# First values of a two-layer decoder trunk projected from the raw first tile, with the norm weights applied by feature

## The chip, the cores and the metric

The kernel runs on one core of a Trainium2 chip. The metric is the device time of one execution in microseconds. Three timed runs of the kernel before gave 706.67, 707.9 and 708.45; one more execution was profiled.

## What is computed

Two decoder layers run over 512 positions of 1024 features. What matters here is the start of layer 0 and the way its three branches share one normalised input:

```python
def rms_norm(x, g):
    y = xf * lax.rsqrt(jnp.mean(xf * xf, axis=-1, keepdims=True) + EPS)
    return y * g
...
h = rms_norm(x, norm_g)                       # norm_g: 1024 weights, one per feature
a_u, a_v, a_g, b_q, b_k, b_v, b_g, m_q, m_g = split_cols(h @ w_in, EVEN_SPLITS)
...
y_m = memory_attention(m_q, mem_n, m_wkv, m_qnorm, m_knorm) * silu(m_g)
return x + concatenate([y_a, y_b, y_m]) @ w_out
```

The factor of a position (its rsqrt) is the same for all features, so a product of one position's row with the weights can take it before the product or after it. The factor of a feature (its norm weight) must come in before the sum over features.

## The kernel before

The 512 positions are four tiles of 128 rows, x_t[0] to x_t[3]. A projection needs the input with features on the partitions, so `h_tile` makes each tile of h in these steps: ScalarE squares it with a running sum (L412), GpSimd makes the factor of each row (`rstd`, L370 and L372), VectorE multiplies the tile by that factor and by the norm weights (L417; the weights stand in `gain0`, one row of 4 KB that a DMA copies to all 128 partitions, L328), TensorE transposes eight blocks of 128x128 (L399), and `split` writes each half of four blocks as two numbers: ScalarE the rounded high part (L376), VectorE the remainder, the low part (L377). Each weight unit of 128x1024 numbers (512 KB, L384) is split in the same way; with an engine given, VectorE makes the low part (L377), without one GpSimd makes it in two instructions of 512 columns (L386 on ScalarE and L389 on GpSimd). A product of two such operands is three matmuls (`mm3`, L402 to L404).

The first projection is `b_v`, the values of the differential attention: 4 tiles by 8 feature blocks by 3, so 96 matmuls of 512 columns, from four weight units that are loaded ahead (`loaded`). The projection for `a_values` follows, 96 more from four further units.

All DMAs are issued by SyncE in one order. At the start this is: two halves of x_t[0], the norm weights, then in turn a weight unit and a tile of x, then three small tables (vec, tab, col). Raw weight units stand in three pages, so a fourth DMA of a unit waits until the low part of an earlier one is made. Pages of SBUF and banks of PSUM are handed out by small allocators (`Arena`), oldest first; a scheduler sets the order of each engine's instructions when the kernel is built, so that a change at one place can shift the order at others.

In the middle of the kernel the fill work of layer 0 ends with the keys and values of the memory tokens for both layers (`mem_kv`); its keys are normalised (`head_norm`, `to_keys`, L517) and transposed. Then `m_attn` (scores L601 and L602, exponentials L607, scaling L609 and L610) is merged with the first part of the output projection (`out_part`), whose products are L402 to L404 again. Around there SyncE also loads the weights of the second norm (`gain1`, L328).

Of the kernel before, what the change touches and what calls it, by code (L numbers as in the profile page):

```python
# [24 lines left out]
F32R = mybir.dt.float32r  # L25
# [6 lines left out]
P = 128  # L32
# [82 lines left out]
def layout(inputs):  # L115

    g = {k: np.asarray(v) for k, v in inputs.items()}
    wall = np.empty((NUNITS, P, DM), np.float32)
    for name, (src, kind, c) in UNITS.items():
        w = g[src]  # L120
        i, cnt = UIDX[name]
        if kind == "t":
            wall[i] = w[:, c:c + P].reshape(KT, P, P).transpose(1, 0, 2).reshape(P, DM)
        elif kind == "n":
            ww = np.concatenate([w[:, a:a + n] for a, n in c], axis=1)
            n = ww.shape[1]
# [12 lines left out]
    col[:, 5:9] = g["l1_c_norm"].reshape(4, P).T  # L139
    col[:, 9:13] = g["l1_c_conv_b"].reshape(4, P).T  # L140
    col[:, 13:137] = g["l1_c_conv_w"].reshape(31, 4, P).transpose(2, 1, 0).reshape(P, 124)
    for j, nm in enumerate("kv"):
        pe = g[f"l1_d_cmp_pos_{nm}"].reshape(16, 2, 64)
        col[:, 137 + 16 * j:153 + 16 * j] = pe.transpose(1, 2, 0).reshape(P, 16)
    w1 = np.stack([g[f"l1_d_cmp_w1_{nm}"].reshape(16, P, P).transpose(1, 0, 2).reshape(P, 2048) for nm in "kv"])
    w2 = np.concatenate([g[f"l1_d_cmp_w2_{nm}"] for nm in "kv"], axis=1)
    wsT = np.ascontiguousarray(g["l0_a_ws"].transpose(2, 0, 1).reshape(P, 512))
    norms = np.stack([g["mem_norm"], g["l0_norm"], g["l1_norm"]])
    return dict(x=g["x"].reshape(S, DM), mem=g["mem"].reshape(256, DM), wall=wall, wqb=wqb,
                vec=vec, bs=g["l0_a_bs"].reshape(1, 512), col=col, w1=w1, w2=np.ascontiguousarray(w2), wsT=wsT, norms=norms,  # L150
                tab=tables())


# [132 lines left out]
def emit(ctx, tc, nc, D, out):  # L286
# [28 lines left out]
    def tok(i):  # L315
        return slice(i * P, (i + 1) * P)
# [15 lines left out]
    x_t[0] = x_sc([P, DM])  # L332
    for a in range(2):
        dma(x_t[0][:, a * 512:(a + 1) * 512], D["x"][tok(0), a * 512:(a + 1) * 512])
    gain0 = load_gain(1, start_sc)
    coff = [0]

    def C(shape):
# [7 lines left out]
            v = v.rearrange("p (a b c) -> p a b c", a=shape[1], b=shape[2])  # L346
        return v

    ident = C([P, P])
    make_identity(nc, ident)  # L350
    mhalf = C([P, 32])
# [16 lines left out]
    def rstd(sc, ss, scale, n, eps=EPS, parts=P):  # L368
        v = sc([P, n])[:parts]
        G.tensor_scalar(v, ss, scale, eps, MUL, ADD)  # L370
        r = sc([P, n])[:parts]
        G.tensor_tensor(r, v, mhalf[:parts, :n], ALU.pow)  # L372
        return r
# [29 lines left out]
        mm(o, lh, rl, start=False, stop=False)  # L403
        mm(o, ll, rh, start=False, stop=last)  # L404

    def h_tile(xt, gain, hs, tk, parts=1):
        with SC() as sc:
            xs = sc([P, DM])
            ss = sc([P, 2])
            cols = [slice(a * DM // parts, (a + 1) * DM // parts) for a in range(parts)]  # L410
            for a, c in enumerate(cols):
                act(xs[:, c], xt[:, c], AF.Square, accum_out=ss[:, a:a + 1])  # L412
            if parts == 2:
                G.tensor_tensor(ss[:, 0:1], ss[:, 0:1], ss[:, 1:2], ADD)
            r = rstd(sc, ss[:, 0:1], 1.0 / DM, 1)
            for c in cols:
                V.scalar_tensor_tensor(xs[:, c], xt[:, c], r, gain[:, c], MUL, MUL)  # L417
            for b in range(2):
                with SC() as pc:
                    p = pc.ps("t", [P, 4, P])  # L420
                    for k in range(4):
                        tr(p[:, k, :], xs[:, (4 * b + k) * P:(4 * b + k + 1) * P])
                    split(p, hs[0][b][:, :, tk], hs[1][b][:, :, tk])
# [18 lines left out]
            w += [(h[:, j * n:(j + 1) * n], l[:, j * n:(j + 1) * n]) for j in range(nk)]  # L442
        return w

    def proj_N(hs, units, order, n, loaded=()):


        order = list(order)
        per = S // n
        groups = [order[a:a + per] for a in range(0, len(order), per)]  # L450
        psc = [SC() for _ in groups]
        ps = [c.ps("d", [P, per, n]) for c in psc]
        k0 = 0
        for m, part in enumerate(units):
            with (loaded[m][0] if m < len(loaded) else SC()) as wsc:
                w = loaded[m][1] if m < len(loaded) else unit_parts(wsc, part, n)
                for a, g in enumerate(groups):
                    for b, i in enumerate(g):
                        for j, (wh, wl) in enumerate(w):
                            k = k0 + j  # L460
                            mm3(ps[a][:, b, :], hs[0][k // 4][:, k % 4, tok(i)], hs[1][k // 4][:, k % 4, tok(i)],
                                wh, wl, k + b == 0, k == KT - 1 and b == len(g) - 1)
                    if k0 + len(w) == KT:
                        for b, i in enumerate(g):
                            yield i, ps[a][:, b, :]
                        psc[a].close()
                k0 += len(w)
# [281 lines left out]
    for i in range(NT):  # L749
        if i:  # L750
            x_t[i] = x_sc([P, DM])
            dma(x_t[i], D["x"][tok(i), :])
        wsc = SC()
        loaded.append((wsc, unit_parts(wsc, first[i], 512, V)))
    dma(vec, bc(D["vec"], [P, VLEN]))
    dma(tab, D["tab"])
    dma(col, D["col"])
    hsc = SC()
    h0 = [[hsc([P, 4, S], F32R) for _ in range(2)] for _ in range(2)]
    for i in range(NT):  # L760
        h_tile(x_t[i], gain0, h0, tok(i), 1 if i else 2)
    x_sc.close()


# [144 lines left out]
    bV = [bsc([P, 2, 512]) for _ in range(2)]  # L909

    def b_v():
        for i, p in proj_N(h0, first, range(NT), 512, loaded):
            act(bV[i // 2][:, i % 2, :], p, AF.Copy)
            yield UT

    yB = [ysc([P, 2, S]) for _ in range(2)]

# [103 lines left out]
                (out_part(0, [(yA[0], 0, 2), (yA[1], 2, 2)], rev), FILLM0)))  # L1021
    msc.close()
    g1sc = SC()
    gain1 = load_gain(2, g1sc)
    banks(*P_DENSE)
    drain(out_part(0, [(yB[0], 4, 2), (yB[1], 6, 2), (yM[0], 8, 2)], rev))
    ysc.close()
# [345 lines left out]
FILLG, FILLC, GLU1 = 0.8, 0.12, 1  # L1373


ARRAYS = ["x", "mem", "wall", "wqb", "vec", "bs", "col", "w1", "w2", "wsT", "norms", "tab"]


def build(shapes):
# [13 lines left out]
```

## Time and profile before

| what | value |
|---|---|
| timed runs | 706.67, 707.9, 708.45 us (median 707.9) |
| profiled execution, its own time | 706.9 us |
| its span in the profile | 705.2 us |
| TensorE busy | 665.2 us, 94% |
| VectorE busy | 492.9 us, 70% |
| ScalarE busy | 376.7 us, 53% |
| GpSimd busy | 392.9 us, 56% |

The span is what the profile shows; 1.7 us of the profiled execution's time lie outside it. TensorE is called PE in rows (PEld is its weight load), VectorE DVE, ScalarE ACT, GpSimd POOL, SyncE SP. A row of a timeline gives start and length in us, then engine, line, operation and operands, and in brackets the idle time ahead of it and what ended that.

### The profile page before, as it was taken

Reading aid. Unit: us, or ns where it says so; the run is one execution under the profiler, and the core shown is the slowest. Engines: PE = TensorE matmul, PEld = TensorE weight load, DVE = VectorE, ACT = ScalarE, POOL = GpSimd, SP = SyncE. Lnnn points to the kernel's source line nnn. Section 1 sums busy time; section 2 is a strip of 40 time slices with the busy share of each in tenths; the row PEclk is TensorE's granted clock in tenths of the full one; section 3 lists DMA queues with packets and bytes.
Section 4 is the critical chain, followed back from the end, with each engine's and each line's share of the span. In section 5 each row is a group of like instructions: output and inputs, shape, how many; then the busy total and the mean of one; then the engine's idle time right before and its main releaser. Section 6 shows DMA issues by size and latency. Waiting matters only on the chain.

```text
span 705.2 us, 11053 instructions
## 1 busy us (share of the span) xinstructions
PE 665.2 (94%) x3819; PEld 563.5 (80%) x3819; DVE 492.9 (70%) x1204; ACT 376.7 (53%) x846; POOL 392.9 (56%) x414
## 2 busy tenths in 40 slices
PE   4999989999999997899999999999999999999997
PEld 3789989888888875688888888777777888788875
DVE  4705678667666865675274978999967776998773
ACT  5345345556455675563253568642446666676541
POOL 3467887575436767442473879966664523421650
PEclk9999999999999999799999999999999999999999
DMA  8532135463313253212132411104121101120121
GB/s 303 187 116 94 60 87 151 140 171 128 108 57 121 90 190 134 95 63 88 51 104 85 151 66 60 61 1 149 32 89 59 61 31 60 51 70 1 61 76 74
DMA packets 22376, 66.56 MB, mean 94 GB/s; under 512 B 3504, under 2 KB 3760, under 8 KB 22320
## 3 DMA queue, kind: packets, MB, share of 16 engines
q1 hardware_dynamic: 22320, 65.86, 28.8%
q8 instruction: 30, 0.49, 0.3%
q14 instruction: 26, 0.21, 0.1%
HBM read 57.46 MB, written 2.10 MB: 84 GB/s over the span
## 4 chain that ended last, share of the span: by engine, by line
PE 71%; DVE 11%; POOL 7%; ACT 4%; DMA 4%; issue 3%; SPq 0%; POOLq 0%; ACTq 0%; DVEq 0%
PE banks L403 18%; PE banks L402 18%; PE banks L404 18%; PE banks L399 5%; PE banks L927 4%; DMA arena_f<-in_wall_dram 3%; POOL arena_r L389 3%; POOL arena_f L372 3%; PE banks L1212 2%; DVE arena_r L377 2%; PE banks L965 2%; ACT arena_r L386 1%; DVE arena_f L929 1%; PE banks L1088 1%; PE banks L1182 1%
## 5 line engine op out<-in xcount | busy, mean ns | idle before, releaser
L389 POOL TENSOR_TENSOR arena_r<-arena_f,arena_r 128x512 fp32r<-128x512 f32 (+1 forms) x174 | 228.5, 1337 | 187.4 <-ACT arena_r L386 183.8
L402 PE MATMUL banks<-arena_r 128*128 128x512 f32 (+2 forms) x784 | 290.0, 374 | 5.1 <-ACT arena_r L386 2.3
L403 PE MATMUL banks<-arena_r 128*128 128x512 f32 (+2 forms) x784 | 289.9, 370 | 3.2 <-POOL arena_r L389 2.1
L404 PE MATMUL banks<-arena_r 128*128 128x512 f32 (+2 forms) x784 | 288.3, 370 | 0.0
L402 PEld LDWEIGHTS banks<-arena_r 128*128 128x128 f32 x784 | 148.4, 190 | 30.3 <-ACT arena_r L386 3.7
L403 PEld LDWEIGHTS banks<-arena_r 128*128 128x128 f32 x784 | 148.7, 190 | 26.9 <-POOL arena_r L389 3.9
L404 PEld LDWEIGHTS banks<-arena_r 128*128 128x128 f32 x784 | 148.4, 189 | 22.6 <-DVE arena_r L377 0.3
L386 ACT ACTIVATE arena_r<-arena_f 128x1024 fp32r<-128x1024 f32 (+2 forms) x87 | 91.2, 1049 | 76.2 <-PE banks L403 21.6
L399 PE MATMUL banks<-const,arena_f 128*128 128x128 f32 x507 | 80.5, 277 | 13.9 <-DVE arena_f L417 9.7
L929 DVE CUSTOM_DVE_ANT_0 arena_f<-banks,const 128x512 f32<-128x512 f32 (+3 forms) x128 | 60.4, 484 | 33.4 <-PE banks L927 26.7
L377 DVE TENSOR_TENSOR arena_r<-banks,arena_r 128x512 fp32r<-128x512 f32 (+1 forms) x112 | 66.8, 608 | 22.9 <-ACT arena_r L376 22.5
L399 PEld LDWEIGHTS banks<-const,arena_f 128*128 128x128 f32 x507 | 60.9, 143 | 25.3 <-DVE arena_f L417 10.2
L376 ACT ACTIVATE arena_r<-banks 128x512 fp32r<-128x512 f32 (+1 forms) x112 | 57.2, 532 | 41.8 <-PE banks L399 28.8
L372 POOL TENSOR_TENSOR arena_f<-arena_f,const 128x4 f32<-128x4 f32 (+3 forms) x60 | 68.0, 1136 | 3.6
L1261 DVE SCALAR_TENSOR_TENSOR banks<-arena_f,const,banks 128x482 f32<-128x482 f32 (+14 forms) x90 | 66.1, 734 | 1.3
L927 PE MATMUL banks<-arena_r 128*128 128x512 f32 (+7 forms) x192 | 50.6, 337 | 4.4 <-DVE arena_f L929 2.1
L958 ACT ACTIVATE arena_f<-arena_f 128x512 f32<-128x512 f32 (+3 forms) x64 | 35.8, 561 | 26.4 <-DVE arena_f L929 25.9
L1189 ACT ACTIVATE arena_f<-arena_f 128x256 f32<-128x256 f32 (+3 forms) x64 | 35.7, 559 | 26.1 <-DVE arena_f L929 25.3
L657 DVE TENSOR_TENSOR arena_f<-arena_f,banks 128x512 f32<-128x512 f32 x40 | 27.0, 684 | 24.0 <-PE banks L404 23.7
L574 POOL TENSOR_SCALAR arena_f<-arena_f 128x512 f32<-128x512 f32 (+3 forms) x32 | 19.9, 627 | 39.6 <-DVE arena_f L1191 33.7
L927 PEld LDWEIGHTS banks<-arena_r 128*128 128x128 f32 (+1 forms) x192 | 32.7, 189 | 10.6 <-DVE arena_f L929 4.7
L1259 POOL TENSOR_TENSOR arena_f<-arena_f 128x482 f32<-128x482 f32 (+29 forms) x30 | 37.8, 1258 | 2.2 <-ACT arena_f L1258 0.6
(177 smaller groups left out, 810.6 us busy)
## 6 DMA issues: line engine op xcount, KB each, us to landing
arena_f<-in_wall_dram SPq DMA_DIRECT2D x88, 512.0 KB, 3.3
arena_r<-arena_r SPq DMA_DIRECT2D x96, 64.0 KB, 2.0
arena_f<-in_x_dram SPq DMA_DIRECT2D x7, 512.0 KB, 6.2
arena_f<-in_w_dram SPq DMA_DIRECT2D x4, 512.0 KB, 3.7
out_dram<-arena_f SPq DMA_DIRECT2D x8, 256.0 KB, 2.0
arena_f<-in_norms_dram SPq DMA_DIRECT2D x3, 512.0 KB, 4.4
arena_f<-in_mem_dram SPq DMA_DIRECT2D x2, 512.0 KB, 3.3
arena_f<-in_wqb_dram SPq DMA_DIRECT2D x2, 420.0 KB, 3.3
```

The costliest lines, as they stand in the source:

```text
L372: G.tensor_tensor(r, v, mhalf[:parts, :n], ALU.pow)
L376: act(h, src, AF.Copy)
L377: (eng or V).tensor_tensor(l, src, f32(h), SUB)
L386: act(h, raw, AF.Copy)
L389: G.tensor_tensor(l[:, c], raw[:, c], f32(h[:, c]), SUB)
L399: nc.tensor.transpose(o, i, ident[:k, :k])
L402: mm(o, lh, rh, start=first, stop=False)
L403: mm(o, lh, rl, start=False, stop=False)
L404: mm(o, ll, rh, start=False, stop=last)
L927: mm(t[:, a % per, :], q, k[:, :w], start=b == 0, stop=b == len(qk) - 1)
L929: V.tensor_tensor_reduce(e[a], t[:, a % per, :], cmask[:, S - w:], -1.0, -NEG, ADD, ALU.min, nm[:, a:a + 1])
L1261: V.scalar_tensor_tensor(acc[:, z:], hc[:, :S - z], cw[:, f, k:k + 1], acc[:, z:], MUL, ADD)
```

## The change

The first tile is transposed raw. `t_tile` transposes four blocks, multiplies them in PSUM by the norm weights, which now stand as a column per feature block in `gcol` (128 partitions by 8, a DMA of 4 KB), and splits them. The first tile goes through it twice: once raw into `own`, which only `b_v` uses, and once multiplied by its row factor into h0 as the others. For the products from `own` the row factor comes in when ScalarE copies the values of tile 0 out of PSUM (`scale=r_first`). For all four tiles the row factor is applied by GpSimd (`G.tensor_scalar`, 128x1024) instead of VectorE, and the norm weights by VectorE after the transposes. The DMA that copied the row of norm weights to all partitions is gone at the start. Of the four weight units of `b_v`, the second and the fourth have their low part made by GpSimd now.

```diff
-    gain0 = load_gain(1, start_sc)
...
+    gcol = C([P, KT])
+    dma(gcol, D["gcol"])
...
+    def t_tile(xs, hs, tk):
+        for b in range(2):
+            with SC() as pc:
+                p = pc.ps("t", [P, 4, P])
+                for k in range(4):
+                    tr(p[:, k, :], xs[:, (4 * b + k) * P:(4 * b + k + 1) * P])
+                V.tensor_tensor(p, p, bc(gcol[:, 4 * b:4 * b + 4].unsqueeze(2), [P, 4, P]), MUL)
+                split(p, hs[0][b][:, :, tk], hs[1][b][:, :, tk])
...
-        loaded.append((wsc, unit_parts(wsc, first[i], 512, V)))
+        loaded.append((wsc, unit_parts(wsc, first[i], 512, None if i % 2 else V)))
...
+    ownsc = SC()
+    own_t = ownsc([P, 4, S], F32R)
+    own = [[own_t[:, 2 * a + b, :].rearrange("p (k t) -> p k t", k=4) for b in range(2)] for a in range(2)]
+    t_tile(x_t[0], own, tok(0))
     for i in range(NT):
-        h_tile(x_t[i], gain0, h0, tok(i), 1 if i else 2)
+        with SC() as sc:
+            xs = sc([P, DM])
+            r = rms(sc if i else ownsc, xs, x_t[i], 1 if i else 2)
+            if i == 0:
+                r_first = r
+            G.tensor_scalar(xs, x_t[i], r, 0.0, MUL, ADD)
+            t_tile(xs, h0, tok(i))
...
-        for i, p in proj_N(h0, first, range(NT), 512, loaded):
-            act(bV[i // 2][:, i % 2, :], p, AF.Copy)
+        for i, p in proj_N(h0, first, range(NT), 512, loaded, own):
+            act(bV[i // 2][:, i % 2, :], p, AF.Copy, scale=1.0 if i else r_first)
```

The order of the instructions changes with it at two places; lines of the changed kernel are a little larger (L399 becomes L401, L402 to L404 become L404 to L406, L377 L379, L389 L391, L372 L374, L384 L386, L328 L329, L324 L325, L601 and L602 become L616 and L617, L517 L532). On TensorE at the start of the program stood, before, eight transposes behind VectorE's scaled tile and then the first products:

```order
L399 MATMUL banks<-const,arena_f 128x128 [waits DVE_49]
L399 MATMUL banks<-const,arena_f 128x128 x3
L402 MATMUL banks<-arena_r 128x512 [waits Activation_49]
L403 MATMUL banks<-arena_r 128x512 [waits DVE_49]
L404 MATMUL banks<-arena_r 128x512 [waits DVE_49]
```

Now the raw tile's transposes wait for the DMA of x alone, and the transposes of the scaled tile come in behind the first product:

```order
L401 MATMUL banks<-const,arena_f 128x128 [waits DMAHW0_49,Pool_49]
L401 MATMUL banks<-const,arena_f 128x128 x3
L401 MATMUL banks<-const,arena_f 128x128 [waits DMAHW1_49]
L401 MATMUL banks<-const,arena_f 128x128 x3
L404 MATMUL banks<-arena_r 128x512 [waits Activation_49]
L401 MATMUL banks<-const,arena_f 128x128 [waits DVE_49,Pool_49]
L401 MATMUL banks<-const,arena_f 128x128 x3
L405 MATMUL banks<-arena_r 128x512 [waits DVE_49]
```

What moved: the first transposes left VectorE's queue, and eight more transposes stand among the products of tile 0. GpSimd, at the same place, had only the row factors (L370, L372) before its first low parts; now its queue holds the row scaling (L786) and the low part of a weight unit (L391) between them:

```order
L374 TENSOR_TENSOR arena_f<-arena_f,const 128x1 [waits Pool_49]
L786 TENSOR_SCALAR arena_f<-arena_f 128x1024 [waits DMAHW1_49,DMAHW0_49,Pool_49]
L372 TENSOR_SCALAR arena_f<-arena_f 128x1 [waits Activation_49]
L374 TENSOR_TENSOR arena_f<-arena_f,const 128x1 [waits Pool_49]
L786 TENSOR_SCALAR arena_f<-arena_f 128x1024 [waits DMAHW4_49,Pool_49]
L391 TENSOR_TENSOR arena_r<-arena_f,arena_r 128x512 [waits DMAHW5_49,Activation_49]
L391 TENSOR_TENSOR arena_r<-arena_f,arena_r 128x512
```

The second place is the entry into the memory attention. On SyncE the load of the second norm's weights stood before a weight unit; before:

```order
L328 DMA arena_f_61<-in_norms_dram 128x1024 [waits PE_49]
L384 DMA arena_f_61<-in_wall_dram 128x1024 [waits DMAHW1_49,DMAHW5_49,Activation_49,Pool_49]
L324 DMA arena_f_61<-in_x_dram 128x1024 [waits DMAHW6_49,PE_49]
```

In the changed kernel that unit is issued ahead of it:

```order
L386 DMA arena_f_61<-in_wall_dram 128x1024 [waits DMAHW1_49,DMAHW4_49,Activation_49,Pool_49]
L329 DMA arena_f_61<-in_norms_dram 128x1024 [waits DMAHW5_49,PE_49]
L325 DMA arena_f_61<-in_x_dram 128x1024 [waits PE_49]
```

On TensorE, behind the first scores (L601 and L602), the second set of scores was followed by the products of the output projection; before:

```order
L601 MATMUL banks<-arena_r 128x256 [waits Activation_49]
L602 MATMUL banks<-arena_r 128x256
L402 MATMUL banks<-arena_r 128x512 [waits DVE_49]
L403 MATMUL banks<-arena_r 128x512 [waits Pool_49]
```

Now four transposes, two sets of scores and four more transposes (those of the memory keys, behind VectorE's L532) stand ahead of these products:

```order
L401 MATMUL banks<-const,arena_f 128x128 [waits DVE_49]
L401 MATMUL banks<-const,arena_f 128x128 x3
L616 MATMUL banks<-arena_r 128x256 [waits Activation_49]
L617 MATMUL banks<-arena_r 128x256
L401 MATMUL banks<-const,arena_f 128x128 [waits DVE_49]
L401 MATMUL banks<-const,arena_f 128x128 x3
L404 MATMUL banks<-arena_r 128x512
L405 MATMUL banks<-arena_r 128x512 [waits Pool_49]
```

## Rows read from the trace of the kernel before

**Rows 1.** The page: busy time of each engine, share of the span, instructions.

```profile
PE 665.2 (94%) x3819; PEld 563.5 (80%) x3819; DVE 492.9 (70%) x1204; ACT 376.7 (53%) x846; POOL 392.9 (56%) x414
```

**Rows 2.** Windows: stretch, its length, busy time by engine, clock, DMA share, GB/s.

```profile
0.00:10.00 10.00, 0.27 (x1) 0.27 (x2) 1.88 (x3) 2.73 (x5) 3.75 (x17) 1.00 0.67 237
...
280.00:290.00 10.00, 4.65 (x15) 3.87 (x16) 5.92 (x14) 6.42 (x16) 8.40 (x12) 0.57 0.55 201
```

**Rows 3.** Timeline of the first 13 us: what leads to the first product.

```profile
5.72 0.57 POOL L372 TENSOR_TENSOR arena_f<-arena_f,const 128x1 f32<-128x1 f32 x1
8.93 1.41 DVE L417 SCALAR_TENSOR_TENSOR arena_f<-arena_f 128x512 f32<-128x512 f32 x2 [6.25 <-DMA arena_f<-in_norms_dram]
9.73 1.97 PE L399 MATMUL banks<-const,arena_f 128*128 128x128 f32 x8 [9.73 <-DVE arena_f L417]
10.07 1.06 ACT L376 ACTIVATE arena_r<-arena_f 128x1024 fp32r<-128x1024 f32 x1 [4.99 <-DMA arena_f<-in_wall_dram]
```

**Rows 4.** DMA from 0 to 30 us: GB/s in 40 slices of 0.75 us; one issue.

```profile
GB/s 0 0 120 382 197 104 109 213 339 344 377 421 421 426 410 421 421 428 409 382 390 388 261 315 377 251 66 126 350 224 104 350 219 38 126 355 284 197 322 180
...
arena_f<-in_vec_dram SPq DMA_DIRECT2D x1, 288.0 KB, 11.0
```

**Rows 5.** Groups by line and form, whole run: count, busy us, mean ns, idle before.

```profile
L377 DVE TENSOR_TENSOR arena_r<-banks,arena_r 128x512 fp32r<-128x512 f32 x80 | 53.9, 684 | 21.7 <-ACT arena_r L376 21.6
L509 DVE TENSOR_TENSOR banks<-banks,const 128x512 f32<-128x512 f32 x4 | 2.8, 691 | 0.0
L377 DVE TENSOR_TENSOR arena_r<-arena_f,arena_r 128x1024 fp32r<-128x1024 f32 x4 | 4.9, 1219 | 0.8 <-ACT arena_r L376 0.8
L574 POOL TENSOR_SCALAR arena_f<-arena_f 128x512 f32<-128x512 f32 x8 | 6.6, 831 | 8.6 <-DVE arena_f L1191 8.1 <-ACT arena_r L535 0.5
L389 POOL TENSOR_TENSOR arena_r<-arena_f,arena_r 128x512 fp32r<-128x512 f32 x171 | 225.6, 1343 | 187.4 <-ACT arena_r L386 183.8 <-PE banks L927 2.9
```

**Rows 6.** Chain that ended last, GpSimd's first low part: start, us.

```profile
23.06 4.24 POOL arena_r L389
```

**Rows 7.** Timeline of VectorE: ten small table instructions (first, last), one behind GpSimd.

```profile
20.57 0.17 DVE L780 TENSOR_SCALAR arena_f<-arena_f 128x32 f32<-128x32 f32 x1
...
21.71 0.14 DVE L807 TENSOR_SCALAR const<-const 128x1 f32<-128x1 f32 x1
...
26.05 1.26 DVE L1275 TENSOR_SCALAR const<-const 128x4 f32<-128x4 f32 x1
```

**Rows 8.** Timeline of TensorE: transposes of later tiles, and 14 products' spacing.

```profile
20.80 0.60 PE L399 MATMUL banks<-const,arena_f 128*128 128x128 f32 x4
...
31.80 1.03 PE L399 MATMUL banks<-const,arena_f 128*128 128x128 f32 x8
...
33.60 0.39 PE L402 MATMUL banks<-arena_r 128*128 128x512 f32 x1
...
36.80 0.39 PE L404 MATMUL banks<-arena_r 128*128 128x512 f32 x1
```

**Rows 9.** Timelines at the entry into the memory attention, by engine.

```profile
274.98 0.33 SPq L328 DMA_DIRECT2D arena_f<-in_norms_dram  x1
...
280.89 1.06 ACT L386 ACTIVATE arena_r<-arena_f 128x1024 fp32r<-128x1024 f32 x1 [1.57 <-DMA arena_f<-in_wall_dram]
...
283.37 1.06 ACT L386 ACTIVATE arena_r<-arena_f 128x1024 fp32r<-128x1024 f32 x1 [0.39 <-DMA arena_f<-in_wall_dram]
...
282.48 0.80 PE L601 MATMUL banks<-arena_r 128*128 128x256 f32 x2 [3.15 <-ACT arena_r L376]
...
287.73 0.58 PE L601 MATMUL banks<-arena_r 128*128 128x256 f32 x1 [2.87 <-ACT arena_f L610]
...
288.75 0.63 PE L402 MATMUL banks<-arena_r 128*128 128x512 f32 x1
...
285.44 1.98 POOL L372 TENSOR_TENSOR arena_f<-arena_f,const 128x4 f32<-128x4 f32 x2
...
290.90 0.69 DVE L517 TENSOR_TENSOR arena_f<-banks,arena_f 128x512 f32<-128x512 f32 x1 [1.22 <-POOL arena_f L372]
```

More of the change, by code (lines that the diff above doesn't have):

```diff
@@ L147, in layout @@
     wsT = np.ascontiguousarray(g["l0_a_ws"].transpose(2, 0, 1).reshape(P, 512))
-    norms = np.stack([g["mem_norm"], g["l0_norm"], g["l1_norm"]])
+    norms = np.stack([g["mem_norm"], g["l1_norm"]])
+    gcol = np.ascontiguousarray(g["l0_norm"].reshape(KT, P).T)
     return dict(x=g["x"].reshape(S, DM), mem=g["mem"].reshape(256, DM), wall=wall, wqb=wqb,
-                vec=vec, bs=g["l0_a_bs"].reshape(1, 512), col=col, w1=w1, w2=np.ascontiguousarray(w2), wsT=wsT, norms=norms,
+                vec=vec, bs=g["l0_a_bs"].reshape(1, 512), col=col, w1=w1, w2=np.ascontiguousarray(w2), wsT=wsT, norms=norms, gcol=gcol,
                 tab=tables())
@@ L404, in mm3, with rms, h_tile @@
         mm(o, ll, rh, start=False, stop=last)
-    def h_tile(xt, gain, hs, tk, parts=1):
+    def t_tile(xs, hs, tk):
[6 more added lines that the diff above has]
+                split(p, hs[0][b][:, :, tk], hs[1][b][:, :, tk])
+    def rms(sc, xs, xt, parts=1):
+        ss = sc([P, 2])
+        cols = [slice(a * DM // parts, (a + 1) * DM // parts) for a in range(parts)]
+        for a, c in enumerate(cols):
+            act(xs[:, c], xt[:, c], AF.Square, accum_out=ss[:, a:a + 1])
+        if parts == 2:
+            G.tensor_tensor(ss[:, 0:1], ss[:, 0:1], ss[:, 1:2], ADD)
+        return rstd(sc, ss[:, 0:1], 1.0 / DM, 1)
+    def h_tile(xt, gain, hs, tk):
         with SC() as sc:
             xs = sc([P, DM])
[L409 to L417, printed above, removed]
+            r = rms(sc, xs, xt)
+            V.scalar_tensor_tensor(xs, xt, r, gain, MUL, MUL)
             for b in range(2):
@@ L443, in unit_parts, with proj_N @@
         return w
-    def proj_N(hs, units, order, n, loaded=()):
+    def proj_N(hs, units, order, n, loaded=(), own=None):
         order = list(order)
@@ L458, in proj_N @@
                     for b, i in enumerate(g):
+                        hi, tk = (own, tok(0)) if own and i == 0 else (hs, tok(i))
                         for j, (wh, wl) in enumerate(w):
                             k = k0 + j
-                            mm3(ps[a][:, b, :], hs[0][k // 4][:, k % 4, tok(i)], hs[1][k // 4][:, k % 4, tok(i)],
+                            mm3(ps[a][:, b, :], hi[0][k // 4][:, k % 4, tk], hi[1][k // 4][:, k % 4, tk],
                                 wh, wl, k + b == 0, k == KT - 1 and b == len(g) - 1)
@@ L911, in b_v @@
     def b_v():
-        for i, p in proj_N(h0, first, range(NT), 512, loaded):
-            act(bV[i // 2][:, i % 2, :], p, AF.Copy)
+        for i, p in proj_N(h0, first, range(NT), 512, loaded, own):
+            act(bV[i // 2][:, i % 2, :], p, AF.Copy, scale=1.0 if i else r_first)
             yield UT
+        ownsc.close()
     yB = [ysc([P, 2, S]) for _ in range(2)]
@@ L1023, in emit @@
     g1sc = SC()
-    gain1 = load_gain(2, g1sc)
+    gain1 = load_gain(1, g1sc)
     banks(*P_DENSE)
@@ L1373 @@
 FILLG, FILLC, GLU1 = 0.8, 0.12, 1
-ARRAYS = ["x", "mem", "wall", "wqb", "vec", "bs", "col", "w1", "w2", "wsT", "norms", "tab"]
+ARRAYS = ["x", "mem", "wall", "wqb", "vec", "bs", "col", "w1", "w2", "wsT", "norms", "gcol", "tab"]
 def build(shapes):
```

## The prediction

> **What bounds the kernel now.** I read the page first: TensorE is busy 94% of the span [rows 1], so a change of some microseconds can only come from its idle time or from work added to it. The table of windows then shows where it idles: 0.27 us of work in the first 10 us, and 4.65 us in 280 to 290, where the granted clock is 0.57, so near the lower of its two levels [rows 2]. These are the two places that the order of instructions changes. The timeline of the start shows the chain: VectorE's L417 sits idle 6.25 us until the norm weights land at 8.93, the first transposes start at 9.73, and the first weight unit lands only at 10.07 [rows 3]. So two things end together, the norm weights and the first weights, and removing the first helps only if the second comes earlier too. The DMA rows say that it can: the rate is 382 GB/s while the first tile comes in, falls to 104 and 109 in the two slices from 3.75 to 5.25 us, and reaches 421 only from 8.25 on [rows 4]. The fall begins where the copies of the one norm row are next in the queues.
>
> **The change at the start, step by step.** The transposes of the raw tile lose their wait for L417. What they feed cannot be used before weights are there, so the first term is the landing of the first unit. Lower bound of the gain: the 0.524 MB of the norm DMA at 421 GB/s, 1.25 us, so 8.8. Upper bound: the first tile ends about 3.8 and one unit of 0.524 MB follows at the same rate, 5.1. I take 6.2, nearer the early end, since the low rate begins with the norm row. The new 4 KB DMA for `gcol` I put at nothing: it has until the transposes end, and if it were as late as the norm row now (8.93) the whole gain of the raw tile were lost.
>
> From there ScalarE's high part takes 1.06 [rows 3], to 7.26. VectorE's low part of this unit takes 1.22 [rows 5]. GpSimd has the row factor at 6.29 [rows 3] and now scales the tile; no row shows 1024 columns. The form of 512 takes 0.83 [rows 5], so it lies between 0.83 and 1.66; I take 1.25, to 7.55. Two rows show that the two engines can hold each other up: GpSimd's first low part took 4.24 us [rows 6] where the mean is 1.34 [rows 5], while VectorE ran small instructions back to back, and then a VectorE instruction on 4 columns took 1.26 [rows 7]. So I let VectorE wait to 7.55, and the unit's low part ends at 8.8. VectorE then has, up to the low part of tile 1's first half: three multiplications in PSUM (0.69 each), four low parts from PSUM (0.68), one low part of a unit (1.22) [rows 5], and the ten small table instructions, 1.3 us from first to last end [rows 7]: 7.3 us. I add 1.5 us of waits, for ScalarE's high parts and for GpSimd, and come to 17.6. (The tables must have landed: vec now needs 11.0 us [rows 4] and is issued behind the same transfers, so it comes as much earlier as the weights.) TensorE transposes the first half of tile 2 into the bank that this frees, at 17.7. Before, the same batch stood at 20.80 [rows 8]. At both points 20 products and all but 16 transposes are done (the 8 extra transposes lie in idle time), so 3.1 us are won here. With no waits on VectorE it is 4.6, with the weights at 8.8 it is 0.5.
>
> Behind it, 41 products and 8 transposes took 11.0 us, where 0.228 for a product and 0.13 for a transpose give 10.4 [rows 8]: 0.6 lost before. In the changed kernel VectorE still owes twelve table instructions, and each may wait for GpSimd, which is now busy with row scaling and the low parts of two units. One such wait is 1.26 at most [rows 7]; I put 1.2 lost in all. Gain of the start: 3.1 - (1.2 - 0.6) = 2.5 us, between -0.5 and 4.5.
>
> The Trainium skill, SBUF — State Buffer, section Who interferes with whom, says that a VectorE instruction contends with a GpSimd instruction that reads SBUF only if it has two SBUF inputs or runs in a two-port mode, and that the loser is blocked for the whole instruction. The trace agrees with the blocking: 4.24 and 1.26 us [rows 6, 7]. By the rule the ten new multiplications in PSUM are free of it, where L417 was not, and the added waits stay at those that I count; if every VectorE instruction contended, ten more waits of up to 1.25 us would turn the gain into a loss.
>
> **The change in the middle.** Nothing of the computation is edited here, but the order is another [rows 9]. Ahead of the memory attention SyncE's load of the second norm's weights was issued at 274.98, and the weight unit behind it arrived for ScalarE at 280.89; TensorE sat idle 3.15 us until 282.48. Now that unit goes first. ScalarE could take it from 279.4 on, 1.5 us earlier. But the next unit (283.37) stays behind both transfers, and ScalarE's high part of it still ends at 284.43. GpSimd's low part of it, 2.7 us [rows 5], now stands ahead of the two instructions for the key factors (1.98 us), which before ran at 285.44. So they end at about 289.5, VectorE's L532 for the first keys runs at about 290.5 to 291, and its transposes stand on TensorE ahead of the output products. These products began at 288.75; now I expect them at 292. Done by then are 4 scores and 8 transposes that came later before: some 0.4 and 1.0 us. Loss: 3.25 - 1.45 = 1.8 us, between a gain of 1.5 (the transfer) and a loss of 4 (if the stall at low clock goes on). What is queued behind the waiting transposes is the output products, and for these VectorE's residual adds wait, with nothing else late.
>
> **Sum.** 706.9 - 2.5 + 1.8 = 706.2 for the profiled execution. The median of the timed runs lies 1.0 above it, so I forecast 707.2: no change that can be told.
>
> **The rivals.** (1) The middle loses nothing: the earlier transfer gives half of its 1.5 us and the waits of the new order overlap with the old idle time (3.15 and 2.87 us [rows 9]). Then 706.9 - 2.5 - 0.8 = 703.6, timed 704.6, faster. For it speaks that TensorE idles there anyway; against it that the transposes now stand ahead of products that were ready.
> (2) Slower: GpSimd's low part of the second unit is held up by VectorE's dense small instructions as its first one was, 4.24 instead of 1.34 [rows 5, 6], on the path of tile 0's next products. That is 2.9 us more at the start, so -0.4 there, and 1.8 in the middle: 709.1, timed 710.1, 0.31% slower. It decides from about 2.8 us of added wait on. For it speaks that GpSimd now has some 14 us of work up to 21 us (four scalings of 1.25, four halves of low parts of 1.34, four factors of about 0.9); against it that the tables land after the second unit's turn.
> The lock of the skill's page named above is the same mechanism.
> (3) The change does not do what it says: the low DMA rate is not the norm row's, the first weights come at 8.8, and the start gives 0. Then 708.7, timed 709.7, still within what the measurement cannot tell.
>
> **How the numbers follow.** A measurement of this kernel tells some 0.3% (2.1 us) from no change. I give my forecast 0.42, rival 1 0.33, rival 2 0.20, rival 3 0.05. Faster holds rival 1, 0.33; slower rival 2, 0.20; the rest is 0.47. The range goes from 703.2 (rival 1 with a start gain of 4) to 711.0 (rival 2 with another microsecond in the middle); my own case has 705.2 to 709.4.
>
> **What the changed profile would show.** Right: TensorE's first transposes at about 3.4, the first unit's high part at about 6.2, the transposes of tile 2's first half near 17.7, and in the middle output products some 3 us later relative to the first scores. Wrong: the first unit after 8; GpSimd's L391 above 3 us at the start; in the middle no idle time of TensorE ahead of the key transposes. The forecast falls by the faster side if the stretch from the first scores to the output products is no longer than before.

## The result and the profile after

The changed kernel is slower: 712.62 us median of six executions (712.57 to 713.64) against 708.45 for the kernel before on the same chip, a ratio of 1.0064 with a 95% interval of 1.0039 to 1.0088. The forecast was 707.2, and its range ended at 711.0. The profiled execution, the slowest of the six, takes 713.64 with a span of 711.9, where the kernel before had 706.9 and 705.2. The two profiles lie further apart than the medians (6.7 against 4.2 us): the six executions of the kernel before range from 706.67 to 711.18, and its profile is near the fast end.

The first line of the page says that the busy time rose by 8.8 us on TensorE, 10.7 on VectorE and 5.7 on GpSimd [rows 1]:

```profile
PE 674.0 (95%) x3827; PEld 570.3 (80%) x3827; DVE 503.6 (71%) x1209; ACT 379.2 (53%) x848; POOL 398.6 (56%) x422
```

Eight more transposes are far from 8.8 us, so TensorE did much of the same work more slowly. The timelines of the start show the gain that was forecast, up to the half tile at 18.68:

```profile
5.60 0.57 POOL L374 TENSOR_TENSOR arena_f<-arena_f,const 128x1 f32<-128x1 f32 x1
...
7.06 1.06 ACT L378 ACTIVATE arena_r<-arena_f 128x1024 fp32r<-128x1024 f32 x1 [1.07 <-DMA arena_f<-in_wall_dram]
...
3.54 1.94 PE L401 MATMUL banks<-const,arena_f 128*128 128x128 f32 x8 [3.54 <-POOL ccm L1149]
8.17 0.80 PE L404 MATMUL banks<-arena_r 128*128 128x512 f32 x1 [2.69 <-ACT arena_r L378]
...
18.68 0.63 PE L401 MATMUL banks<-const,arena_f 128*128 128x128 f32 x4 [0.94 <-DVE arena_r L379]
```

The weights are taken at 7.06 instead of 10.07 [rows 3], the first product comes at 8.17, and the transposes of tile 2's first half at 18.68 instead of 20.80 [rows 8]: 2.1 us won. Then it is lost. The next rows are VectorE's, GpSimd's, ScalarE's and TensorE's between 18 and 28 us:

```profile
18.52 1.03 DVE L841 TENSOR_SCALAR const<-const 128x4 f32<-128x4 f32 x1
...
19.59 1.37 DVE L812 TENSOR_TENSOR const<-arena_f 128x128 f32<-128x128 f32 x1
...
20.99 1.37 DVE L812 TENSOR_TENSOR const<-arena_f 128x128 f32<-128x128 f32 x1
...
23.20 1.27 DVE L813 TENSOR_TENSOR const<-arena_f 128x64 f32<-128x64 f32 x1
...
24.52 0.68 DVE L415 TENSOR_TENSOR banks<-banks,const 128x512 f32<-128x512 f32 x1
...
18.36 1.16 POOL L786 TENSOR_SCALAR arena_f<-arena_f 128x1024 f32<-128x1024 f32 x1
19.49 6.12 POOL L391 TENSOR_TENSOR arena_r<-arena_f,arena_r 128x512 fp32r<-128x512 f32 x4
...
25.24 0.60 ACT L378 ACTIVATE arena_r<-banks 128x512 fp32r<-128x512 f32 x1 [0.40 <-DVE banks L415]
...
25.89 0.59 PE L404 MATMUL banks<-arena_r 128*128 128x512 f32 x1 [2.92 <-ACT arena_r L378]
...
27.13 0.63 PE L406 MATMUL banks<-arena_r 128*128 128x512 f32 x1
27.56 0.63 PE L404 MATMUL banks<-arena_r 128*128 128x512 f32 x1
```

Four of VectorE's small table instructions take over a microsecond each, always beside a GpSimd instruction that reads SBUF (the first beside the row scaling, three beside the low parts). Behind them stands tile 1's second multiplication L415, which starts only at 24.52; ScalarE's high part waits for it, and TensorE stands still for 2.92 us. In the kernel before, TensorE's longest wait between 20 and 30 us was 0.43:

```profile
27.34 0.50 PE L403 MATMUL banks<-arena_r 128*128 128x512 f32 x1 [0.43 <-POOL arena_r L389]
```

After the stall of 2.92 us the products are 0.43 us apart (27.13 to 27.56) instead of 0.23: the clock has fallen. The windows view shows it here and at three other places; its columns are those of [rows 2]:

```profile
20.00:30.00 10.00, 7.08 (x26) 5.44 (x26) 8.16 (x18) 2.09 (x4) 5.61 (x4) 0.83 0.50 179
90.00:100.00 10.00, 7.55 (x55) 7.27 (x54) 7.27 (x27) 2.98 (x8) 9.25 (x9) 0.89 0.31 75
280.00:290.00 10.00, 6.14 (x28) 4.84 (x27) 6.64 (x14) 7.08 (x17) 9.51 (x14) 0.78 0.82 271
290.00:300.00 10.00, 8.87 (x32) 7.08 (x31) 6.15 (x15) 5.20 (x16) 3.96 (x4) 0.54 0.29 99
495.00:505.00 10.00, 7.93 (x29) 5.61 (x29) 8.59 (x17) 1.74 (x4) 3.48 (x5) 0.83 0.40 153
```

A mean of 0.83 over 10 us is 3.4 us at the lower level (1.2 instead of 2.4 GHz). In the profile of the kernel before, the first, the second and the last of these stretches have 1.00, and of the five only those around 285 us hold the lower level [rows 2]:

```profile
20.00:30.00 10.00, 9.56 (x47) 7.51 (x46) 8.72 (x33) 2.90 (x5) 5.62 (x3) 1.00 0.72 216
90.00:100.00 10.00, 7.88 (x66) 7.60 (x65) 6.25 (x23) 3.65 (x9) 7.69 (x9) 1.00 0.39 93
495.00:505.00 10.00, 9.36 (x40) 7.13 (x40) 9.38 (x22) 2.50 (x5) 6.12 (x9) 1.00 0.17 54
```

**Where the 6.7 us went.** Where TensorE's order is the same in both kernels, one instruction can be looked up in both timelines, and the difference of its times is how far the changed kernel is behind. Two such pairs; first the kernel before, then the changed one:

```profile
94.77 0.47 PE L927 MATMUL banks<-arena_r 96*128 96x512 f32 x1 [2.12 <-DMA arena_r<-arena_r]
...
494.06 0.73 PE L402 MATMUL banks<-arena_r 128*128 128x512 f32 x2 [1.53 <-ACT arena_r L386]
```

```profile
97.10 0.47 PE L954 MATMUL banks<-arena_r 96*128 96x512 f32 x1 [2.45 <-DMA arena_r<-arena_r]
...
499.63 0.73 PE L404 MATMUL banks<-arena_r 128*128 128x512 f32 x2 [1.36 <-ACT arena_r L388]
```

97.10 - 94.77 = 2.33, of which 0.33 is a longer wait for a DMA. Read so along the whole trace, at places where the order agrees, the changed kernel is 2.0 us behind at 60 us, 3.8 at 105 (the low clock from 98 on lies between), 3.8 at 172, 5.7 at 400 (the middle), 6.8 at 520 (the low clock behind the second pair) and 6.8 at the end. So the start lost 2.0 where 2.5 were to be won, the middle lost 1.85 (1.8 forecast), and two stretches of low clock that no step of the sum had cost 1.8 and 1.1.

In the middle the rows are TensorE's, SyncE's and GpSimd's; they answer to [rows 9]:

```profile
284.82 0.50 PE L616 MATMUL banks<-arena_r 128*128 128x256 f32 x2 [1.47 <-ACT arena_r L378]
...
289.36 1.11 PE L401 MATMUL banks<-const,arena_f 128*128 128x128 f32 x4 [2.17 <-DVE arena_f L1007]
...
293.75 1.11 PE L401 MATMUL banks<-const,arena_f 128*128 128x128 f32 x4 [0.80 <-DVE arena_f L532]
294.52 0.78 PE L404 MATMUL banks<-arena_r 128*128 128x512 f32 x1
...
279.12 0.33 SPq L386 DMA_DIRECT2D arena_f<-in_wall_dram  x1
279.54 0.38 SPq L329 DMA_DIRECT2D arena_f<-in_norms_dram  x1
...
286.19 2.49 POOL L391 TENSOR_TENSOR arena_r<-arena_f,arena_r 128x512 fp32r<-128x512 f32 x2
...
289.47 2.50 POOL L391 TENSOR_TENSOR arena_r<-arena_f,arena_r 128x512 fp32r<-128x512 f32 x2
291.93 2.03 POOL L374 TENSOR_TENSOR arena_f<-arena_f,const 128x4 f32<-128x4 f32 x2
```

From the first scores to the output products it is 294.52 - 284.82 = 9.7 us; before it was 288.75 - 282.48 = 6.3 [rows 9]. Low parts of weight units stand ahead of the factors on GpSimd (2.49 and 2.50 us), and both batches of transposes come late by it: TensorE waits 2.17 us for L1007 (the last scaling of the differential attention) and 0.80 for L532.

### The profile page after: what moved, and what is told of

The parts are those of the page before. It is cut to its first block, busy times and chain, and to the rows that moved or that the text cites. A ratio compares the mean times of both kernels' runs of the same rounds, so it can differ in the third digit from the quotient of the medians.

```text
span 711.9 us, 11088 instructions
## 1 busy us (share of the span) xinstructions
PE 674.0 (95%) x3827; PEld 570.3 (80%) x3827; DVE 503.6 (71%) x1209; ACT 379.2 (53%) x848; POOL 398.6 (56%) x422
## 4 chain that ended last, share of the span: by engine, by line
PE 72%; DVE 12%; POOL 7%; ACT 3%; issue 2%; DMA 2%; SPq 0%; POOLq 0%; ACTq 0%; DVEq 0%
PE banks L405 18%; PE banks L404 18%; PE banks L406 18%; PE banks L401 6%; PE banks L954 4%; POOL arena_r L391 3%; POOL arena_f L374 3%; DVE arena_r L379 2%; PE banks L1239 2%; DMA arena_f<-in_wall_dram 2%; PE banks L992 2%; ACT arena_r L388 1%; PE banks L1115 1%; DVE arena_f L956 1%; PE banks L1209 1%
## 5 line engine op out<-in xcount | busy, mean ns | idle before, releaser
L391 POOL TENSOR_TENSOR arena_r<-arena_f,arena_r 128x512 fp32r<-128x512 f32 (+1 forms) x178 | 230.4, 1319 | 191.8 <-ACT arena_r L388 180.0
L404 PE MATMUL banks<-arena_r 128*128 128x512 f32 (+2 forms) x784 | 292.7, 376 | 10.4 <-ACT arena_r L378 5.6
L406 PE MATMUL banks<-arena_r 128*128 128x512 f32 (+2 forms) x784 | 290.3, 372 | 0.0
L404 PEld LDWEIGHTS banks<-arena_r 128*128 128x128 f32 x784 | 149.8, 192 | 36.3 <-ACT arena_r L378 7.4
L405 PEld LDWEIGHTS banks<-arena_r 128*128 128x128 f32 x784 | 150.3, 192 | 25.4 <-POOL arena_r L391 3.3
L406 PEld LDWEIGHTS banks<-arena_r 128*128 128x128 f32 x784 | 150.2, 192 | 22.4
L388 ACT ACTIVATE arena_r<-arena_f 128x1024 fp32r<-128x1024 f32 (+2 forms) x89 | 93.3, 1050 | 82.4 <-PE banks L406 23.4
L401 PE MATMUL banks<-const,arena_f 128*128 128x128 f32 (+1 forms) x515 | 84.4, 282 | 11.6 <-POOL ccm L1149 3.5
L378 ACT ACTIVATE arena_r<-banks 128x512 fp32r<-128x512 f32 (+1 forms) x114 | 58.8, 534 | 48.1 <-PE banks L401 29.3
L401 PEld LDWEIGHTS banks<-const,arena_f 128*128 128x128 f32 (+1 forms) x515 | 63.7, 146 | 24.6 <-POOL ccm L1149 3.5
L379 DVE TENSOR_TENSOR arena_r<-banks,arena_r 128x512 fp32r<-128x512 f32 (+1 forms) x114 | 68.6, 610 | 15.3 <-ACT arena_r L378 14.8
L374 POOL TENSOR_TENSOR arena_f<-arena_f,const 128x4 f32<-128x4 f32 (+3 forms) x60 | 68.4, 1143 | 3.5
L985 ACT ACTIVATE arena_f<-arena_f 128x128 f32<-128x128 f32 (+3 forms) x64 | 35.8, 561 | 27.4 <-DVE arena_f L956 26.8
```

Source lines behind the costliest of these rows:

```text
L378: act(h, src, AF.Copy)
L379: (eng or V).tensor_tensor(l, src, f32(h), SUB)
L388: act(h, raw, AF.Copy)
L391: G.tensor_tensor(l[:, c], raw[:, c], f32(h[:, c]), SUB)
L401: nc.tensor.transpose(o, i, ident[:k, :k])
L404: mm(o, lh, rh, start=first, stop=False)
```

## The experiments

Theory A says that VectorE's table instructions are held up by GpSimd's low parts, and that tile 1 stands behind them. Theory B says that VectorE simply has too much work of its own. C says that the order in the middle costs what it cost; D that its loss comes of the shift in time. E and F are two readings of the falls of the clock: they belong to the changed order, or they come wherever a shift puts the same idle time. The table gives the microseconds behind the kernel before (minus: ahead), read as above from each profile; a dash where the order differs. Medians and ratios are of the timed executions, against the kernel before on the same chip.

| kernel | median us (runs) | ratio, interval | 60 us | 105 | 172 | 400 | 520 |
|---|---|---|---|---|---|---|---|
| changed | 712.62 (6) | 1.0064, 1.0039 to 1.0088 | +2.0 | +3.8 | +3.8 | +5.7 | +6.8 |
| e1 | 707.63 (10) | 0.9999, 0.9980 to 1.0019 | -3.7 | -3.6 | -3.6 | -1.4 | 0.0 |
| e2 | 713.09 (5) | 1.0067, 1.0030 to 1.0105 | +0.8 | +2.6 | +2.6 | +4.8 | +6.0 |
| e3 | 709.35 (10) | 1.0016, 0.9995 to 1.0038 | -2.4 | -1.8 | -1.9 | -0.4 | +0.8 |
| e4 | 714.74 (4) | 1.0101, 1.0033 to 1.0168 | +0.1 | - | - | +7.9 | +9.2 |
| e5 | 708.41 (10) | 0.9985, 0.9958 to 1.0012 | -0.9 | +0.6 | +2.2 | +1.9 | +3.7 |
| e6 | 709.85 (10) | 1.0017, 0.9993 to 1.0041 | +1.0 | +2.6 | +2.5 | +2.5 | +4.2 |
| e7 | 708.42 (10) | 0.9993, 0.9963 to 1.0022 | -3.5 | -2.0 | -0.5 | +1.0 | +1.9 |
| e8 | 703.20 (7) | 0.9913, 0.9883 to 0.9944 | -4.1 | -2.4 | - | -2.3 | -2.4 |
| e9 | 716.87 (1) | none | -1.4 | - | - | +8.6 | +9.9 |
| e10 | 711.42 (10) | 1.0035, 1.0012 to 1.0059 | -1.3 | -0.9 | - | -0.7 | -0.8 |
| e11 | 708.29 (10) | 1.0002, 0.9977 to 1.0026 | -0.1 | +1.6 | - | +2.4 | +2.4 |
| e12 | 705.15 (10) | 0.9952, 0.9933 to 0.9971 | -2.5 | -2.5 | - | -2.4 | -2.4 |

**e1, tables late.** The changed kernel; three copies of one column make the loads of the tables wait for the last tile of h.

```diff
-    dma(vec, bc(D["vec"], [P, VLEN]))
-    dma(tab, D["tab"])
-    dma(col, D["col"])
...
     drain(b_v())
+    for t in (vec, tab, col):
+        act(t[:, 0:1], f32(h0[0][1])[:, 3, S - 1:S], AF.Copy)
+    dma(vec, bc(D["vec"], [P, VLEN]))
+    dma(tab, D["tab"])
+    dma(col, D["col"])
...
+    bcg, bsg = rope_tables("cosb", "sinb", "bq", "bk", 32.0 ** -0.5, 32, 8)
...
     drain(a_values())
```

> The changed kernel with the three small tables (vec, tab, col) loaded, and VectorE's table instructions run, only after the last tile of h is split. The order on TensorE in the middle stays that of the changed kernel. Theory A (at the start VectorE's table instructions stand ahead of tile 1's second multiplication L415 and are held up by GpSimd's low parts): the 2.92 us stall of TensorE at 25.9 goes, and with it the low clock from 26.2 to 29.6; at 45 us the kernel is 2 to 3 us ahead of the kernel before instead of 2.0 behind; 705.5 to 709 us, by whether the clock falls again later. Theory B (VectorE simply has too much work of its own from the second pass of the first tile): a stall of 2 us or more stays, at 45 us still 0.5 us or more behind, 711 or more.

The stall near 26 and its low clock are gone; at 60 us the kernel is 3.7 ahead, 5.7 better than the changed one. It gives 2.2 back in the middle and 1.4 at a fall of the clock near 493, so its time is that of the kernel before. That the tables' place costs the start is shown; whether by their own time or by being held up, not yet.

**e2, low parts on VectorE.**

```diff
-        loaded.append((wsc, unit_parts(wsc, first[i], 512, None if i % 2 else V)))
+        loaded.append((wsc, unit_parts(wsc, first[i], 512, V)))
```

> The changed kernel with the low parts of all four loaded weight units on VectorE again, tables where they are. Theory A: GpSimd's pair of low parts at 11.7 and half of its four at 19.5 go; VectorE has 2.4 us more of its own work but fewer instructions that are blocked, so the lag behind the kernel before at 45 us falls from 2.0 to between 0 and 1.5. Theory B (VectorE's own work binds): 2.4 us more on VectorE make the lag 3.5 or more, 714 or more.

+0.8 at 60 us, as A has it: 2.4 us more work on VectorE made the start 1.2 us better. But TensorE now waits for VectorE's low parts, once for 2.0 us, with the lower clock behind it (0.83 in the mean from 20 to 30 us), and twice for 1.3 us together; so its own work is not far behind as a bound.

**e3, no raw tile.**

```diff
-    t_tile(x_t[0], own, tok(0))
...
-        for i, p in proj_N(h0, first, range(NT), 512, loaded, own):
-            act(bV[i // 2][:, i % 2, :], p, AF.Copy, scale=1.0 if i else r_first)
+        for i, p in proj_N(h0, first, range(NT), 512, loaded):
+            act(bV[i // 2][:, i % 2, :], p, AF.Copy)
```

> The changed kernel without the raw pass of the first tile: values of tile 0 come from the scaled tile as those of the others; 8 transposes, 2 multiplications and 2 low parts on VectorE are gone. Theory A: the blocked table instructions stay, the stall of about 3 us near 26 stays, lag at 45 us 1.5 to 3. Theory B: VectorE has 2.7 us less to do, the stall shrinks below 1 us, lag at 45 us below 0.

This fell out as B said, 2.4 ahead; A alone is not enough. The raw pass costs this start 4.4 us, more than its 2.7 us on VectorE. The rows show why both hold: without it the tables run earlier, and tile 1's second multiplication comes at 20.92, when GpSimd's four low parts (19.58) have only begun:

```profile
20.92 0.69 DVE L415 TENSOR_TENSOR banks<-banks,const 128x512 f32<-128x512 f32 x1
...
19.58 5.08 POOL L391 TENSOR_TENSOR arena_r<-arena_f,arena_r 128x512 fp32r<-128x512 f32 x4
```

**e4, the norm row behind the first unit, in the kernel before.**

```diff
-    gain0 = load_gain(1, start_sc)
...
         loaded.append((wsc, unit_parts(wsc, first[i], 512, V)))
+        if i == 0:
+            gain0 = load_gain(1, start_sc)
```

> The kernel before with one edit: the row of norm weights is loaded behind the first weight unit instead of ahead of it. TensorE's order in the middle then comes out as in the changed kernel, all else as before. Theory C (the order in the middle costs what it cost in the changed kernel): between 270 and 345 us this kernel loses 1.4 to 1.9 us against the kernel before. Rival D (the middle's loss comes of the time by which the changed start shifts everything, not of the order): it loses less than 0.5 there. At the start the first unit should be taken by ScalarE at about 7.1, as in the changed kernel, and the norm row lands about 1 us later, so 0.5 to 1.5 us behind at 45 us. Total: C 709 to 710.5, D 707.5 to 708.5, both without further falls of the clock.

ScalarE took the first unit at 7.81 instead of 10.07, so the norm row did hold the weights. At 60 us this kernel is 0.1 behind, where 0.5 to 1.5 was expected, and its time of 714.74 lies above both forecasts. From 270 to 400 us it lost 3.3, with one fall of the clock inside. But TensorE's order differed between 95 and 270 us too, which the expectation did not say, and this cost 4.6 more, two falls of the clock included. For the size of C it is inconclusive.

**e5, tables late in the kernel before.** The edit of e1, with memory of its own for the row of norm weights.

> The kernel before with one edit, the same as in e1: vec, tab and col are loaded, and VectorE's table instructions run, only after the last tile of h is split. From the 164th instruction of TensorE on its order is that of the kernel before to the end, so the middle should lose nothing. Theory A (the start is bound by VectorE's queue, in which table instructions meet GpSimd's low parts): the tables took VectorE 3 us between 20.6 and 24.9, TensorE waited little behind them (0.43 us), so the gain at 45 us is 0.3 to 1.5 us; 706.5 to 707.6 if the clock falls nowhere else. Theory E (falls of the clock at about 97 and 500 belong to the changed order in the middle): none there. Theory F (they come wherever a shift of a microsecond or two puts the same idle time): one or both appear, 1.1 to 1.8 us each.

0.9 won at the start, and then two falls of the clock that the profiled execution of the kernel before does not have, at 95 and at 498 us, although TensorE's order is the same from its 164th instruction on. So E is out: the falls need no changed order. F holds in so far as they come here with a shift of the start alone; that a shift always brings them is not shown, and e12 below, 2.5 us ahead, has neither. A third one at 167 us cost 1.6.

**e6, two low parts on GpSimd in the kernel before.** The edit of e2 the other way round.

> The kernel before with one edit: the low parts of the second and the fourth loaded weight unit on GpSimd, as in the changed kernel. TensorE's order from its 164th instruction on is that of the kernel before. Theory A: GpSimd's low parts now run beside VectorE's scaling L417 and beside its table instructions, each of which is held up by up to 1.3 us; what VectorE saves (2 x 1.22) is lost again, lag at 45 us between 0 and +2. Theory B (VectorE's own work alone binds): 2.4 us less of it, so 1 to 2.4 us ahead at 45 us. Theories E and F on the clock as for the kernel before with late tables.

1.0 behind at 60 us, where B had 1 to 2.4 ahead: taking 2.4 us of work from VectorE made the start slower. The clock fell at 96 and 499 us again.

**e7, no raw tile and tables late.** The edits of e1 and e3.

> The changed kernel with the tables late (as e1) and without the raw pass of the first tile (as e3). If the raw pass pays once the tables are out of its way, this kernel is slower at 45 us than e1, which was 3.7 us ahead of the kernel before: by the first product, which comes about 2 us later without it, 1.5 to 2.5 us ahead. If the raw pass is only a load on VectorE, it is 3.7 to 5 us ahead. The order in the middle is that of the changed kernel, so it loses 1.4 to 2.2 us there; total 705 to 710 with one or two falls of the clock.

3.5 ahead against e1's 3.7: near the case in which the raw pass is only a load on VectorE, far from the 2 us of an earlier first product.

**e8, e1 with another order in the middle.**

```diff
-FILL0, FILL1, FILLM0, FILLM1, FILLQ = 3.1, 2.67, 2.9, 4.52, 2.6
+FILL0, FILL1, FILLM0, FILLM1, FILLQ = 3.2, 2.67, 2.9, 4.52, 2.6
```

> e1 with the pace of the fill work in the differential attention at 3.2 instead of 3.1. By that the order on TensorE from its 894th to its 1845th instruction is another one, in which output products stand ahead of the memory attention's second scores, nearly as in the kernel before. Theory C (the order in the middle costs 1.4 to 2.2 us): between 270 and 345 us it loses less than 0.7 against the kernel before, so 3 us ahead from there on; 703 to 705 if the clock falls nowhere else. Rival: the middle loses as much in another place, 706 or more.

The start is that of e1, and from 105 to 400 us it loses 0.1 instead of 2.2, as C has it. This is the fastest kernel of the study, 0.9913 of the kernel before.

**e9, GpSimd's low parts of 8 columns.** Six low parts are cut short, the rest of them is zero.

```diff
+                if left:
+                    V.memset(f32(l), 0.0)
...
+                    if left:
+                        c = slice(a, a + left.pop())
                     G.tensor_tensor(l[:, c], raw[:, c], f32(h[:, c]), SUB)
```

> The changed kernel in which GpSimd's first six low parts (the second and fourth loaded unit and the first unit of a_values) cover 8 columns instead of 512 each; the rest of these low parts is left at zero, so part of the products is left out of the result. VectorE's table instructions stay where they are, ahead of tile 1's multiplications. Theory A (VectorE loses its time blocked by GpSimd's low parts): the 128x128 table instructions take 0.28 instead of 1.37, the stall of TensorE near 26 is under 1 us and no low clock follows it, at 45 us 2.5 to 5 us ahead of the kernel before. Theory B (VectorE's own work): the 20 table instructions cost their own 2.5 us all the same, and a stall of 1.5 us or more stays; at 45 us no more than 1 us ahead.

VectorE's table instructions still stand ahead of tile 1's second multiplication, here L421, but they are not held up:

```profile
18.12 0.28 DVE L818 TENSOR_TENSOR const<-arena_f 128x128 f32<-128x128 f32 x1
...
19.03 0.28 DVE L818 TENSOR_TENSOR const<-arena_f 128x128 f32<-128x128 f32 x1
...
21.69 0.68 DVE L421 TENSOR_TENSOR banks<-banks,const 128x512 f32<-128x512 f32 x1
```

0.28 instead of 1.37, no wait of TensorE above 0.8 us behind the first product, no low clock in the first 90 us, 1.4 ahead at 60 us. So it is being held up that makes the stall, as A has it. But 1.4 lies between what A (2.5 to 5) and B (at most 1) gave, and both count: without the waits the start is 3.4 us better than in the changed kernel, the lower clock behind the stall included, and e1, in which the tables' own work is out of the way too, is another 2.3 better. TensorE's order differs here from its tenth instruction on, so the 3.4 need not be of the waits alone; e10, next, has the order of the changed kernel at the start. (The later columns say nothing of this.)

**e10, the changed kernel with the pace of e8.**

> The changed kernel with the pace 3.2 instead of 3.1, tables where they are; from its 166th instruction on TensorE's order is that of e8. Theory A and C: start 2.0 us behind the kernel before as in the changed kernel, and from there to the end as e8, in which the stretch from 105 to 520 us lost nothing: 2 to 4 us behind, by one fall of the clock at about 97; 708.5 to 711.

The median is as expected or a little above it. But the profiled execution is the fastest of ten, with a span of 704.3 where the others have 708.0 to 713.8. Up to 150 us all engines have the order of the changed kernel, and yet it is 1.3 ahead at 60 us instead of 2.0 behind. The rows say why:

```profile
19.00 0.15 DVE L841 TENSOR_SCALAR const<-const 128x4 f32<-128x4 f32 x1
...
19.20 0.28 DVE L812 TENSOR_TENSOR const<-arena_f 128x128 f32<-128x128 f32 x1
...
20.88 0.68 DVE L415 TENSOR_TENSOR banks<-banks,const 128x512 f32<-128x512 f32 x1
...
18.85 2.89 POOL L786 TENSOR_SCALAR arena_f<-arena_f 128x1024 f32<-128x1024 f32 x1
21.70 5.02 POOL L391 TENSOR_TENSOR arena_r<-arena_f,arena_r 128x512 fp32r<-128x512 f32 x4
```

Here GpSimd was the one held up: its row scaling took 2.89 instead of 1.16, VectorE ran through, and the low parts began 2.2 us later. In this execution both engines came to the place half a microsecond later than in the changed kernel's: L841 starts 0.15 us behind the row scaling (19.00, 18.85), there 0.16 (18.52, 18.36), and the other one won. So with one and the same order the start differs by 3.3 us at 60 us, near the 3.4 of e9, by which of the two engines waits. Only this execution of e10 was profiled; the other nine took 3.7 to 9.5 us longer, and their start was not seen.

**e11, the kernel before with the pace of e8.**

> The kernel before with the pace 3.2 instead of 3.1 and nothing else. If e8 gained only by its start (4 us ahead at 60 us), this kernel is as fast as the kernel before, 706.5 to 709. If the new order also gained in the middle by itself, 704 to 706.

No change that can be told: the pace alone is not what makes e8 fast.

**e12, e8 without the raw tile.** The edits of e3 and e8.

> e8 without the raw pass of the first tile (tables late, pace 3.2, values of tile 0 from the scaled tile); from its 149th instruction on TensorE's order is that of e8. At 45 to 60 us e7 stood 0.2 us behind e1, so if the raw pass is worth nothing once the tables are late, this kernel is the same as e8: 703 to 704.5. If it is worth the 2 us by which the first product comes earlier, 705 to 706.

Its interval overlaps that of e8 from above, and at 60 us it is 1.6 behind e8, where e7 was 0.2 behind e1. With the tables out of the way the raw pass is worth something between nothing and 2 us; more can't be told here.

## Why the prediction was wrong

- **First unit at 6.2, low part at 8.8.** 7.06 and 9.4 in the trace. Too early by 0.9 and 0.6, the mechanism is right: e4 moved the norm row alone, and the weights came 2.3 us earlier. Rival 3 is out.
- **Tile 2's first half at 17.7, 3.1 us won.** 18.68, 2.1 won. The chain of VectorE was followed in the right order. (The ten small table instructions of [rows 7] are twelve; their 1.3 us is right, so the sum stands.)
- **"I put 1.2 lost in all" behind it.** This step failed. The sum had 0.6 more lost than before, and it was 2.0 + 2.1 = 4.1: a stall of 2.92 where before 0.43 stood, so 2.5, and the rest, about 1.6, for the 3.4 us of low clock behind it. I had a row for one wait of 1.26 [rows 7] and took it for the whole, though twelve instructions were to pass a queue of four low parts. Four of the twelve waited, one behind the other (1.03 for the row scaling, then 1.37, 1.37 and 1.27): 5.0 us, where the same four took 0.9 in e10. Ahead of them a group of four had already taken 1.34 instead of 0.50. The clock was no term of the start at all, though [rows 2] showed what a stall can do to it.
- **Rival 2 had the mechanism with the roles reversed.** GpSimd's first pair of low parts ran unhindered (2.52 us for two); VectorE was the one held up. That the price of 2.9 us is also the length of the stall is luck: it was worked out from one GpSimd instruction, and the start came out 4.5 us worse than forecast, not 2.9. The rule of the Trainium skill, SBUF — State Buffer, section Who interferes with whom, is borne out: L415, whose large operands lie in PSUM, took 0.68 beside GpSimd's low parts, while four instructions on SBUF took over 1. (Three of these have two inputs in SBUF; L841 has one, and no row shows whether it ran in the two-port mode that the rule then asks for.) The section also says that the order of issue decides which engine blocks; the changed kernel and e10 show both outcomes of one order. What I drew from the rule, that the added waits stay at those that I counted, did not follow from it.
- **The middle, 1.8 lost.** 1.85 in the trace, from 172 to 400 us; the order is the cause, as forecast, but that the number agrees is in part luck, since two errors cancel in it. The first scores came 284.82 - 4.0 = 280.8 on the clock of the kernel before, so 1.7 earlier (1.5 forecast); the output products at 290.5, 1.8 later than 288.75, where I had 3.25. So the delay was 1.45 smaller than forecast, and the 1.45 of work done ahead was hardly credited. The lower level lasted longer (0.77 in the mean from 270 to 300 us against 0.83), but e3 and e7 have 0.83 as well and still lose 1.5, so most of the missing credit stays open. What the order does is plainer: from the first scores to the output products the changed kernel, e1, e2, e3 and e7 take 9.7 to 9.9 us, the kernel before, e5 and e6 6.3. From 172 to 400 us the kernels with this order (e1, e2, e3, e7) lose 1.5 to 2.2; e5 and e6, which come there over 2 us late with the order of before, none, so D is out; e8, e10 and e12 from 105 on 0.1 to 0.2 (e11 0.8, with a fall of the clock at 246 inside).
- **Nothing elsewhere.** The sum has no other term, but the falls of the clock at 98 and 500 us cost 1.8 and 1.1. No part of the change touches these places.
- **The signs of being wrong** did not appear: the first unit came at 7.06, the longest L391 of the start took 2.21 us, and TensorE did sit idle ahead of the key transposes (0.80). None of them was on VectorE's queue, where the step failed.

Why the clock falls behind such an idle stretch in one execution and not in the next is not settled. Open too is how often the start goes as in the profiled execution: the six of the changed kernel lie within 1 us of each other, e10's ten within 9.5.

## What to carry to other kernels

Before work is moved to GpSimd, look at what VectorE will run beside it: many small instructions on SBUF can each pay up to one whole GpSimd instruction (here up to 1.37 us beside low parts of about 1.3), so count the waits by instructions, and see what stands behind the last of them. Here letting small preparatory work wait until the urgent chain was through won 5.7 us at 60 us (e1), of which the end of the program kept something only with another order in the middle (e8). And when TensorE is 94% busy, an edit at the start should be judged at two points, where the stage ends and where the program ends, since a reordered stage and the clock can take back a gain of some microseconds 200 us later.

## What was not expected of the hardware

- The same two idle stretches of TensorE, at about 95 us (2.1 to 2.7 us, for a DMA) and 495 us (1.3 to 2.0 us), are in all 14 profiles. In 8 of them the lower clock followed the first, in 9 the second, and the length of the idle time does not decide it: 2.68 in e3 without, 2.12 in e5 with it. Each cost 1 to 2 us.
- So executions of one kernel differ by their clock. The 73 of the kernel before beside these runs have spans of 703.8 to 711.5 with mean granted clocks of 0.995 to 0.981; a straight line through them gives 6 us for 0.01 of clock. The six of the changed kernel have 0.9865 in the mean against 0.9908: 0.0043, by that line 2.6 of the 4.3 us by which the mean spans differ (711.1 and 706.8); this is an estimate.
- Which of two engines loses at a shared place can be decided by so little that one order gives 2.0 us behind and 1.3 us ahead: the two engines came 0.16 and 0.15 us apart.
